# A list scheduler gets new costs: a shared memory port, other matmul steps, and a price for changing the array's form

## The chip, the cores and the metric

The kernel runs on one core of one Trainium2 chip. Five engines matter: TensorE (PE in the profile; its weight loads are PEld) multiplies matrices into PSUM, VectorE (DVE), ScalarE (ACT) and GpSimd (POOL) work element by element, and SyncE (SP) issues the transfers. The metric is the device time of one execution in microseconds. Times are medians of several runs.

## The reference

One layer of a hybrid decoder on 1024 prompt tokens and 8 x 4 sample tokens, 1056 columns in all, of width 1024, in float32:

- RMSNorm, then one input projection into q (8 heads of 64), k and v (2 heads of 64) and 512 channels for a state-space layer (S5).
- Sliding-window attention (window 128) with sinks and a relative bias, in eight blocks of 128 queries, each against its own and the previous block; the samples attend to a cache.
- S5: 32 groups of 16 channels drive a 64-dimensional diagonal complex state each; a scan over the positions; y = Re(C h) + D u; GELU and a half-GLU.
- RMSNorm of both parts, one output projection, residual; RMSNorm, an MLP of width 4096 with squared ReLU, residual; the final RMSNorm.

The outputs are y for all tokens, the new keys and values, and the new states.

## The kernel before

**Layout.** Activations are held with channels on the 128 partitions and the 1056 tokens along the row, so that a matmul takes a 128x128 weight tile and 352 token columns (`TB`). A float32 product is made of three float32r matmuls: each operand is split into a high and a low part, and high x high, high x low and low x high are summed in PSUM (`mm`, `mm3`). In the profile those are the groups `PS<-R,wh` and `PS<-R,wl`; the text calls them bulk matmuls. A weight tile `wr` (128x512) arrives by DMA, `weights` copies its high part to `wh` (ScalarE or VectorE) and puts the rest into `wl` (VectorE or GpSimd). There are two buffers of each. The other matmuls are plain float32 ones (two records each in the profile) or float32r ones of attention: transposes, score products (`64*128`), value products (`128*64`), the S5 tables, and sums over partitions for the norms.

**Stages.** The kernel is recorded in program order: x and its split, the attention and S5 tables, the input projections (`proj`, `proj_b`), S5 in four generators of eight groups (`s5`), attention (`att_sample`, `att_block`), the attention half of the output projection (`x2_first`), `gelu`, `glu`, the S5 half (`x2_last`), and the MLP (`up`, `down`) with the final norm. The string `SCRIPT` gives the order of record up to the MLP, a token for each piece: the two projections `b2` and `b3`, of 72 bulk matmuls each, stand among the attention steps `A`, with a negative `BOOST`, as fillers for TensorE.

**The planner.** What is recorded is not issued in that order. `Plan.record` notes each operation with its alternatives (an elementwise operation on SBUF tiles, `ew`, may go to VectorE or GpSimd; a copy, `copy`, to ScalarE or VectorE), a cost for each by `op_cost`, and its dependences. `Plan.schedule` then runs a list schedule: `prio` is the longest path of costs to the end; at each step every engine offers the operation that can start earliest (`s`, the later of the engine's free time and the operands' arrival), ties go to the higher priority, and the earliest of the engines' offers is placed. On TensorE, priorities are those of a group of matmuls, with 100 added for all that is not bulk. An operation with alternatives is left for another engine when that one would end it earlier, its waiting queue counted by half (`QW`). Buffers and PSUM banks are given out on the way. `Plan.issue` then writes the operations out in the planned order: each engine's queue is fixed, and only semaphores for true dependences and buffers hold it at run time. All planned operations are issued from one line, so the profile shows them as L339, and groups are told apart by tiles.

**What the planner assumes before the change.** VectorE and GpSimd never disturb each other. A bulk matmul of 352 columns costs 0.0025 + 352/2400 = 0.149 us; a plain one of 64 output rows and n columns 0.03 + n/1200; changing from one kind of matmul to another costs nothing. A VectorE operation of n elements costs 0.07 + n/960 us, a GpSimd one 0.15 + 0.0021 n, or 0.00166 n where an operand is broadcast.

**Names that the prediction uses.** GELU (`gelu`): per group a square, two products with (1 + tanh), one of 1024 and one of 32 columns a row in strided order, and the split. x2_first adds x to an accumulator `big` by `ett(acc[m], acc[m], xr, OP.add)`, a 128x1056 add for VectorE or GpSimd. In S5, the rotated states are put into a row `HA` together with the samples' start states (`pcopy`) and zeros (`ew.memset`), which the y^T products of 136 columns read.

Of the kernel before, what the change touches and what calls it, by code (L numbers as in the profile page):

```python
# [18 lines left out]
# ---------------------------------------------------------------- planning: the kernel is written in program order, its  # L19
# operations are recorded, and a list scheduler puts them in the order in which they are issued  # L20
# [17 lines left out]
class View:  # L38
    """part of a planned tile: the elements it covers, and how the real tile gives it"""
# [33 lines left out]
class Op:  # L73
    __slots__ = ("alts", "tiles", "succ", "ndep", "prio", "avail", "i", "table", "src", "why", "s", "boost", "bulk")


QW = 0.5
# [4 lines left out]
TABLE = {AF.Exp: 1, AF.Tanh: 1, AF.Sin: 2, AF.Sqrt: 3}  # L82


def op_cost(eng, method, args, kw):
    out = args[0]
    if eng == "SP":
        v = next((x for x in args if isinstance(x, View)), None)
        return max(0.1, (v.ix.size if v else math.prod(out.shape)) * 4 / 360e3)
    n = math.prod(out.ix.shape[1:])  # L90
    vs = [a for a in args if isinstance(a, View)]
    psum = any(a.tile.space == "PS" for a in vs)
    if eng == "PE":
        m = args[1].ix.shape[-1]
        if method == "transpose":
            return 0.109
        if args[1].dt == F32R:
            return 0.0025 + max(n, 256) / 2400
        if m <= 64:
            return max(0.06, 0.03 + n / 1200)  # L100
        return max(0.134, 0.0025 + n / 600)
    if eng == "ACT":
        aps = sum(isinstance(kw.get(k), View) for k in ("scale", "bias"))
        return (0.05 if psum else 0.093) + n / 1200 + 0.094 * aps + (0.095 if "accum_out" in kw else 0)
    if eng == "DVE":
        if method == "memset":
            return 0.05
        if method == "reciprocal":
            return 0.07 + n * 0.0062
        if method == "tensor_reduce":  # L110
            n = math.prod(args[1].ix.shape[1:])
        if method in ("tensor_scalar", "tensor_copy") and not psum:
            return 0.07 + n / 1920
        return (0.13 if psum and method == "scalar_tensor_tensor" else 0.07) + n / 960
    if method == "memset":
        return 0.04 + n / 3000
    if method == "tensor_scalar":
        return 0.16 + n / 1200
    bc = len(vs) < 3 or any(a.ix.strides[-1] == 0 for a in vs[1:])
    return 0.15 + n * (1.66 if bc else 2.1) / 1000  # L120


class Plan:
# [4 lines left out]
    # -- tiles  # L128
# [11 lines left out]
    # -- operations  # L140
# [3 lines left out]
    def record(self, calls):  # L144
        o = Op()
        o.i, o.boost, o.bulk = len(self.ops), self.boost, self.bulk
        o.alts = [(e, m, a, k, op_cost(e, m, a, k)) for e, m, a, k in calls]
        a, k = calls[0][2:]
# [3 lines left out]
        f = a[2] if len(a) > 2 else None  # L152
# [18 lines left out]
        if calls[0][0] == "PE":  # L171
            # accumulation groups of a bank stay in order
            v = a[0]
            key = v.box()[2] // 512
            prev = v.tile.last.get(key)
            if prev is not None and o.i not in prev.succ:
                prev.succ[o.i] = False
                o.ndep += 1
            v.tile.last[key] = o
# [7 lines left out]
    # -- the list scheduler  # L187
    def schedule(self):
# [5 lines left out]
        # a group of matmuls counts as its most urgent one  # L194
        group = {}
# [6 lines left out]
        table = [0]  # L202
        pend = {e: [] for e in ENG}
        units_end = {}
        phase_left = [sum(1 for t in self.tiles if t.left and t.phase == p) for p in (0, 1, 2)]
        # allocation: in the order of record among the tiles that compete for a unit
# [21 lines left out]
        def slot(t):  # L228
            """(time, units) of the best free place, or None"""
            if t not in heads[t.space] or (t.phase == 2 and phase_left[1]):  # L230
                return None
            best = None
            for c in t.cands:
                if all(live.get((t.space, u)) is None for u in c):
                    e = max(units_end.get((t.space, u), 0.0) for u in c)
                    if best is None or e < best[0]:
                        best = (e, c)
            return best
# [5 lines left out]
        def queue(e, o):  # L244
            """what is ahead of o on an engine"""
            return self.qw * sum(b[4] for q, b in pend[e] if q.prio > o.prio and q.avail <= free[e])
# [5 lines left out]
        while len(seq) < len(ops):  # L252
            best = None
            for e, lst in pend.items():
                cand = None
                fe = free[e]
                for o, a in lst:
                    s = max(fe, o.avail)
                    if cand is not None and s > cand[0] + 1e-9:
                        continue  # L260
                    if len(o.alts) > 1:
                        fin = s + a[4]
                        if any(b[0] != e and max(free[b[0]], o.avail) + b[4] + queue(b[0], o) < fin for b in o.alts):
                            continue
# [33 lines left out]
            if e == "SP":  # L298
                free[e] = s + 0.5
                dma[0] = max(dma[0], s + 0.5) + a[4]  # L300
                end = dma[0]
            else:
                c = a[4]
                if e == "ACT" and o.table and o.table != table[0]:
                    table[0] = o.table
                    c += 1.28
                end = free[e] = s + c
            for t in o.tiles:
# [22 lines left out]
    # -- issue  # L331
# [33 lines left out]
# rows: which ones a part of the kernel takes  # L365
# [6 lines left out]
# order of record up to the MLP  # L372
# [5 lines left out]
def body(tc, I, O, dbg=None):  # L378
# [14 lines left out]
    def copy(out, in_):  # L393
        """ScalarE or VectorE"""
        plan.record([("ACT", "activation", (out, in_, AF.Copy), {}), ("DVE", "tensor_copy", (out, in_), {})])
# [15 lines left out]
    with ExitStack() as ctx:  # L411
# [57 lines left out]
        # ------------------------------------------------------------ weights: four k-tiles of 128 columns at a time  # L469
# [8 lines left out]
        def mm(outs, w, xs, first, last, cols=tbs):  # L478
            """accumulates sum_k w[k]^T x[k]; three products carry float32"""
# [13 lines left out]
        # ------------------------------------------------------------ constants  # L493
# [11 lines left out]
        # ------------------------------------------------------------ norms: 1/sqrt(mean + eps), per token  # L505
        def rs_sum(ss, p, blocks, start=True, stop=True, b0=0, p0=0):
            """per-token mean of squares (ss summed over partitions), tokens on partitions"""
# [5 lines left out]
        def rs_calc(p, b0, b1, f, out, root=True, p0=0):  # L513
            """out[:, b] = (f sum + eps)^(-1/2), or ^(-1)"""
# [20 lines left out]
        def rs_row(r, row, b0=0, b1=9):  # L535
            """r[token] on all partitions, into a row"""
# [11 lines left out]
        # ------------------------------------------------------------ x: gain, split, squares  # L548
# [32 lines left out]
        # ------------------------------------------------------------ attention tables  # L581
# [36 lines left out]
        # ------------------------------------------------------------ S5 parameters, [(parity, p), pair]  # L618
# [26 lines left out]
        def s5_params():  # L645
# [55 lines left out]
            # (lambda_bar - 1) / lambda  # L701
# [17 lines left out]
            # b_bar and the block diagonal C  # L719
# [5 lines left out]
            # phase tables e^(i 8 theta n): n = 16 a + b  # L725
# [19 lines left out]
        # ------------------------------------------------------------ S5, eight groups (four pairs) at a time  # L745
# [7 lines left out]
        def u_part(ut, b, p):  # L753
            """tokens by s, then n, of 8 n + s; the samples' (i, b) at the end"""
# [12 lines left out]
        def s5(m, units, par):  # L767
            """rows (7 - s, c) of U hold token 8 n + s of channel c; par: rows it is given"""
# [5 lines left out]
            # lambda^s b_bar  # L774
# [9 lines left out]
            # kernel K[tau], its Toeplitz form by way of DRAM; F by transposes  # L784
# [19 lines left out]
            # phase table  # L804
# [6 lines left out]
            # G: Re(C lambda^(t+1)), -Im  # L811
# [25 lines left out]
            # X = F^T U; rotate  # L837
# [47 lines left out]
            # scan  # L885
# [8 lines left out]
            # rotate back  # L894
# [18 lines left out]
            # y^T  # L913
# [19 lines left out]
        # ------------------------------------------------------------ input projection  # L933
# [29 lines left out]
        def in_first(ms):  # L963
            """as x arrives"""
# [14 lines left out]
        def proj_b(m):  # L979
            """by token blocks"""  # L980
# [8 lines left out]
        def kv_tokens():  # L989
            """token-major k (last 128 and sample) and v"""  # L990
# [20 lines left out]
        # ------------------------------------------------------------ attention  # L1011
# [11 lines left out]
        def softmax(S):  # L1023
            """exponentials and their sums"""
# [6 lines left out]
        def probs(S, dn):  # L1031
            """normalized and transposed"""
# [123 lines left out]
        # ------------------------------------------------------------ output projection, residual  # L1156
        ms = [None] * 8

        def o_split(i):
            """o with its gain, in two parts of tokens"""  # L1160
# [27 lines left out]
        # ------------------------------------------------------------ GELU, GLU  # L1188
# [74 lines left out]
        # ------------------------------------------------------------ up to the MLP, in this order  # L1263
# [24 lines left out]
        # ------------------------------------------------------------ MLP; the norm's 1/(mean + eps) comes after the square  # L1288
# [37 lines left out]
        # the last chunk by token blocks, the final norm behind it  # L1326
# [141 lines left out]
```

## Time and profile before

| | us |
|---|---|
| median of 3 runs | 1217.54 |
| lowest, highest | 1208.55, 1219.12 |
| span of the profiled execution, first to last instruction | 1209.6 |
| TensorE busy in it | 1153.0 (95%) |
| VectorE busy | 670.9 (55%) |
| ScalarE busy | 274.2 (23%) |
| GpSimd busy | 277.0 (23%) |

The profile is of one execution; the page gives its span, and no other time of its own. Busy shares are means over the whole span, and the stages differ: the first third holds projections, S5 and attention, the rest the MLP. A busy TensorE is not one at its peak, since matmuls overlap; the granted clock (PEclk, a share of full speed) has two levels, 1.2 and 2.4 GHz, and a mean between 0.5 and 1 tells how the stretch was divided. A name such as `R` stands for a row buffer of 128x1088, `big` for the accumulators, `PS` for PSUM, `t` for a 128x512 scratch, `sx` for small softmax sums. The arrow in a wait points from the waiting instruction to the engine and tile that ended the wait.

### The profile page before, as it was taken

The page shows a single profiled execution, that of the slowest core. Times are in us where ns is not written, and L with a number is a line of the kernel's source. Part 1 is how long each engine was busy: PE and PEld are TensorE (multiplying, and loading weights), DVE is VectorE, ACT ScalarE, POOL GpSimd, SP SyncE. Part 2 cuts the span into 40 slices and gives each one's busy share as a digit, 9 for nine tenths or more (in the row PEclk, how much of TensorE's full clock was granted, in tenths as well). Part 3 has the DMA queues.
Part 4 walks back from the last instruction along what each step waited for, and adds up shares of the span by engine and source line. Part 5 has one row for each costly group of instructions (what it writes and reads, how often), then busy time and mean ns, then how long its engine had stood idle before and what let it go on. Part 6 is the DMA issues. An engine that isn't in the chain of part 4 may idle for free.

```text
span 1209.6 us, 17482 instructions
## 1 busy us (share of the span) xinstructions
PE 1153.0 (95%) x7231; PEld 1109.0 (92%) x7231; DVE 670.9 (55%) x970; ACT 274.2 (23%) x512; POOL 277.0 (23%) x259
## 2 busy tenths in 40 slices
PE   6989999979888999999999999999999999999997
PEld 6888996658778999999999999999999999999996
DVE  8687747898789894522522533432432432534575
ACT  4212134632143321211111111111111111111241
POOL 4066414575463140020010010010011011000011
PEclk9989989969889999999999999999999999999997
DMA  6312320023331111111211111111111211121212
GB/s 234 102 47 71 98 46 11 9 47 93 85 99 44 37 44 43 44 44 44 53 44 45 53 44 36 52 44 44 53 44 45 53 44 44 44 52 44 79 54 92
DMA packets 55711, 69.71 MB, mean 58 GB/s; under 512 B 12184, under 2 KB 31808, under 8 KB 55616
## 3 DMA queue, kind: packets, MB, share of 16 engines
q1 hardware_dynamic: 55632, 68.59, 20.3%
q8 instruction: 57, 0.93, 0.4%
q14 instruction: 22, 0.18, 0.0%
HBM read 58.96 MB, written 6.15 MB: 54 GB/s over the span
## 4 chain that ended last, share of the span: by engine, by line
PE 69%; DVE 3%; ACT 1%; issue 0%; DVEq 0%; ACTq 0%; POOL 0%
PE PS L339 69%; DVE R L339 2%; DVE big L339 1%; ACT P L339 1%; ACT wh L339 0%; ACT R L339 0%; DVE wl L339 0%; DVE rsc L339 0%; DVE wh L339 0%; DVEq L1464 0%; ACT rsc L339 0%; ACTq L339 0%; DVE rs L339 0%; POOL R L339 0%; DVEq L339 0%
## 5 line engine op out<-in xcount | busy, mean ns | idle before, releaser
L339 PE MATMUL PS<-R,wh 128*128 128x352 f32 x3840 | 749.2, 326 | 19.4 <-DVE wh L339 10.1
L339 PEld LDWEIGHTS PS<-R,wh 128*128 128x128 f32 x3840 | 643.2, 191 | 25.6 <-DVE wh L339 10.5
L339 PE MATMUL PS<-R,wl 128*128 128x352 f32 x1920 | 430.1, 326 | 0.9 <-POOL wl L339 0.5
L339 PEld LDWEIGHTS PS<-R,wl 128*128 128x128 f32 x1920 | 331.5, 191 | 4.8 <-issue 2.1
L339 POOL TENSOR_TENSOR wl<-wr,wh 128x512 fp32r<-128x512 f32 x64 | 92.7, 1449 | 700.2 <-ACT wh L339 490.0
L339 ACT ACTIVATE wh<-wr 128x512 fp32r<-128x512 f32 x144 | 91.0, 632 | 649.9 <-PE PS L339 637.4
L339 DVE TENSOR_TENSOR wl<-wr,wh 128x512 fp32r<-128x512 f32 x96 | 70.2, 731 | 255.4 <-ACT wh L339 249.9
L339 DVE TENSOR_TENSOR big<-PS,big 128x1056 f32<-128x1056 f32 (+2 forms) x80 | 82.5, 1035 | 167.0 <-PE PS L339 166.9
L339 PE MATMUL PS<-R,R 128*128 128x384 f32 (+9 forms) x816 | 140.8, 342 | 19.1 <-DVE R L339 8.4
L339 PEld LDWEIGHTS PS<-R,R 128*128 128x128 f32 (+3 forms) x816 | 111.3, 196 | 40.2 <-POOL R L339 15.4
L339 DVE TENSOR_TENSOR R<-R,R 64x508 f32<-64x508 f32 (+8 forms) x55 | 44.6, 823 | 4.9 <-ACT R L339 4.3
L339 POOL TENSOR_TENSOR R<-R,R 128x512 f32<-128x512 f32 (+6 forms) x34 | 39.3, 1163 | 32.6 <-DVE R L339 23.9
L339 DVE TENSOR_TENSOR P<-P 128x1056 f32<-128x1056 f32 x32 | 40.3, 1259 | 6.6 <-ACT P L339 6.6
L339 DVE TENSOR_TENSOR P<-P,R 128x1056 f32<-128x1056 f32 x32 | 40.4, 1263 | 0.9
L339 DVE TENSOR_TENSOR R<-P,R 128x1056 fp32r<-128x1056 f32 x32 | 40.3, 1258 | 1.1
L339 ACT ACTIVATE R<-PS 128x512 f32<-128x512 f32 (+3 forms) x40 | 22.6, 570 | 75.9 <-PE PS L339 70.0
L339 ACT ACTIVATE P<-PS 128x1056 f32<-128x1056 f32 (+2 forms) x35 | 34.6, 988 | 8.8 <-PE PS L339 8.8
L339 ACT ACTIVATE R<-R 128x352 f32<-128x352 f32 (+4 forms) x32 | 25.8, 823 | 38.8 <-DVE R L339 38.5
L339 DVE SCALAR_TENSOR_TENSOR R<-R,R 128x352 f32<-128x352 f32 (+5 forms) x28 | 32.2, 1186 | 1.3 <-ACT R L339 1.3
L339 ACT ACTIVATE R<-R,sx 128x129 f32<-128x129 f32 x68 | 26.5, 392 | 22.7 <-DVE sx L339 22.7
L339 ACT ACTIVATE P<-big 128x384 f32<-128x384 f32 (+2 forms) x29 | 19.1, 662 | 50.5 <-DVE big L339 46.1
L339 POOL TENSOR_TENSOR big<-big,R 128x1056 f32<-128x1056 f32 x7 | 25.8, 3680 | 10.1 <-DVE big L339 9.9
(140 smaller groups left out, 691.1 us busy)
## 6 DMA issues: line engine op xcount, KB each, us to landing
wr<-in_w_up_dram SPq DMA_DIRECT2D x64, 256.0 KB
wr<-in_w_down_dram SPq DMA_DIRECT2D x64, 256.0 KB
R<-in_xT_dram SPq DMA_DIRECT2D x15, 528.0 KB
wr<-in_w_in_dram SPq DMA_DIRECT2D x20, 256.0 KB
wr<-in_w_out_dram SPq DMA_DIRECT2D x16, 256.0 KB
out_y_dram<-big SPq DMA_DIRECT2D x8, 384.0 KB
R<-R SPq DMA_DIRECT2D x32, 68.0 KB
R<-R SPq DMA_DIRECT2D x32, 64.0 KB
```

The costliest lines, as they stand in the source:

```text
L339: getattr(engines[e], m)(*[res(x) for x in args], **{k: res(x) for k, x in kw.items()})
```

## The change

Comments and docstrings are taken out, so that later line numbers shift. Beyond that only the planner is changed; what is recorded, `SCRIPT`, `BOOST` and the buffers stay.

- `op_cost`: new figures for matmuls, for GpSimd's two-input operations, and a factor of 1.87 on a VectorE operation with an operand whose elements lie 8 or more apart (`far`).
- `port`: says whether an operation takes the port that VectorE and GpSimd share: every GpSimd operation but a memset; on VectorE those with two SBUF inputs, the scan, and copies and scalar operations from SBUF to SBUF. `record` notes it (`o.port`), and `schedule` starts such an operation no earlier than the other engine's last such operation ends (`held`), also where it compares alternatives.
- `form`: rows and columns of the array that a matmul's stationary operand takes, rounded up to 32, 64 or 128. A matmul whose form differs from that of the one placed before it starts 0.2 us later in the plan (`SWITCH`).

```diff
-QW = 0.5
+QW, SWITCH = 0.5, 0.2
...
+def far(v):
+    st = [abs(b) for n, b in zip(v.ix.shape, v.ix.strides) if n > 1]
+    return bool(st) and st[-1] >= 8 * v.ix.itemsize
+
+def form(args):
+    up = lambda n: 32 if n <= 32 else 64 if n <= 64 else 128
+    return up(args[1].ix.shape[0]), up(args[1].ix.shape[-1])
...
         if args[1].dt == F32R:
-            return 0.0025 + max(n, 256) / 2400
+            return max(0.056, 0.0133 + n / 2400)
         if m <= 64:
-            return max(0.06, 0.03 + n / 1200)
-        return max(0.134, 0.0025 + n / 600)
+            return max(0.107, n / 600)
+        return max(0.224, 0.013 + n / 600)
...
-        return (0.13 if psum and method == "scalar_tensor_tensor" else 0.07) + n / 960
+        slow = 1.87 if any(far(a) for a in vs) else 1.0
+        return (0.13 if psum and method == "scalar_tensor_tensor" else 0.07) + n / 960 * slow
...
-    bc = len(vs) < 3 or any(a.ix.strides[-1] == 0 for a in vs[1:])
-    return 0.15 + n * (1.66 if bc else 2.1) / 1000
+    return 0.16 + n * 1.75 / 1000
+
+def port(eng, method, args):
+    if method == "memset" or eng not in ("DVE", "POOL"):
+        return False
+    if eng == "POOL":
+        return True
+    big = [a for a in args[1:] if isinstance(a, View) and a.ix.size > a.ix.shape[0]]
+    sb = [a for a in big if a.tile.space != "PS"]
+    if method in ("tensor_scalar", "tensor_copy"):
+        return len(sb) == len(big) and args[0].tile.space != "PS"
+    return len(sb) > 1 or method == "tensor_tensor_scan"
...
+        o.port = {c[0] for c in calls if port(c[0], c[1], c[2])}
+        o.form = form(calls[0][2]) if calls[0][0] == "PE" else None
...
+        held = {"DVE": 0.0, "POOL": 0.0}
+        other = {"DVE": "POOL", "POOL": "DVE"}
+        shape = [None]
...
                     s = max(fe, o.avail)
+                    if e in o.port:
+                        s = max(s, held[other[e]])
+                    if e == "PE" and o.form != shape[0]:
+                        s += SWITCH
...
-                        if any(b[0] != e and max(free[b[0]], o.avail) + b[4] + queue(b[0], o) < fin for b in o.alts):
+                        if any(b[0] != e and max(free[b[0]], o.avail, held[other[b[0]]] if b[0] in o.port else 0.0) + b[4]
+                               + queue(b[0], o) < fin for b in o.alts):
...
                 end = free[e] = s + c
+                if e in o.port:
+                    held[e] = end
+                if e == "PE":
+                    shape[0] = o.form
```

## Rows read from the trace of the kernel before

**Rows 1.** Table by stretches: us, each engine's busy time (instructions), granted clock, DMA share, GB/s.
```profile
0.00:160.00 160.00, 139.96 (x933) 133.52 (x936) 117.31 (x265) 43.59 (x63) 69.62 (x106) 0.95 0.38 108
160.00:270.00 110.00, 100.90 (x640) 73.21 (x622) 88.76 (x154) 50.55 (x179) 55.51 (x50) 0.88 0.10 25
270.00:393.00 123.00, 105.19 (x646) 98.83 (x642) 105.50 (x130) 36.51 (x57) 59.59 (x43) 0.91 0.31 79
393.00:1183.80 790.80, 790.03 (x4929) 787.51 (x4930) 346.01 (x390) 139.19 (x205) 88.02 (x58) 1.00 0.17 47
1183.80:1209.60 25.80, 16.88 (x115) 15.98 (x114) 13.29 (x33) 4.40 (x10) 4.22 (x4) 0.73 0.30 107
```

**Rows 2.** Waits of TensorE, 0 to 393 us: us in total, times, longest.
```profile
PE PS L339 <- POOL R L339: 13.2, 7, 6.0
PE PS L339 <- DVE R L339: 11.6, 7, 4.5
PE PS L339 <- DVE wh L339: 10.1, 2, 5.7
```

**Rows 3.** VectorE's groups by shape, 0 to 393 us: count, busy us, mean ns, idle before.
```profile
L339 DVE TENSOR_TENSOR R<-R,R 128x512 f32<-128x512 f32 x13 | 15.0, 1185 | 0.0
L339 DVE SCALAR_TENSOR_TENSOR R<-R,prm,R 128x1056 fp32r<-128x1056 f32 x7 | 14.5, 2091 | 0.1
L339 DVE TENSOR_TENSOR t<-L,R 128x512 f32<-128x512 f32 x11 | 13.6, 1239 | 0.2
L339 DVE SCALAR_TENSOR_TENSOR R<-R,R 128x32 f32<-128x32 f32 x4 | 9.6, 2403 | 0.0
L339 DVE TENSOR_TENSOR R<-PS,R 128x512 f32<-128x512 f32 x12 | 7.5, 677 | 0.0
```

**Rows 4.** GpSimd's groups by shape, 0 to 393 us.
```profile
L339 POOL TENSOR_TENSOR big<-big,R 128x1056 f32<-128x1056 f32 x7 | 25.8, 3680 | 10.1 <-DVE big L339 9.9
L339 POOL TENSOR_TENSOR R<-R,cst 128x512 f32<-128x512 f32 x14 | 19.2, 1375 | 13.1 <-ACT R L339 9.5 <-DVE R L339 2.0 <-DVE sx L339 1.5
L339 POOL TENSOR_TENSOR R<-R,sx 128x512 f32<-128x512 f32 x12 | 14.9, 1242 | 21.0 <-DVE sx L339 21.0
```

**Rows 5.** VectorE's groups by shape, 450 to 1150 us.
```profile
L339 DVE TENSOR_TENSOR R<-wr,R 128x512 fp32r<-128x512 f32 x6 | 4.1, 689 | 0.1
```

**Rows 6.** Order of time, 0 to 32 us: start us, us, engine, operation, count.
```profile
10.15 1.32 DVE L339 SCALAR_TENSOR_TENSOR R<-R,prm,R 128x1056 fp32r<-128x1056 f32 x1
...
14.60 7.04 DVE L339 SCALAR_TENSOR_TENSOR R<-R,prm,R 128x1056 fp32r<-128x1056 f32 x3
...
14.83 3.41 POOL L339 TENSOR_TENSOR R<-R,R 128x1056 f32<-128x1056 f32 x1 [13.61 <-DVE R L339]
```

**Rows 7.** Order of time, 330 to 366 us, VectorE, then GpSimd.
```profile
333.97 4.51 DVE L339 SCALAR_TENSOR_TENSOR R<-R,R 128x1024 f32<-128x1024 f32 x2
339.70 1.26 DVE L339 TENSOR_TENSOR R<-R,R 128x1056 fp32r<-128x1056 f32 x1 [1.21 <-ACT R L339]
...
334.11 4.30 POOL L339 TENSOR_TENSOR big<-big,R 128x1056 f32<-128x1056 f32 x1
```

**Rows 8.** Order of time, 304 to 320 us.
```profile
311.51 3.29 POOL L339 TENSOR_TENSOR R<-R,R 128x512 f32<-128x512 f32 x2 [1.94 <-DVE R L339]
...
316.19 1.25 PE L339 MATMUL PS<-R,R 128*128 128x136 f32 x4 [6.00 <-POOL R L339]
```

**Rows 9.** Order of time, TensorE, 186 to 200 us and 296 to 304 us.
```profile
188.12 0.32 PE L339 MATMUL PS<-R,wh 128*128 128x352 f32 x1
188.37 4.32 PE L339 MATMUL PS<-R,R 64*128 64x256 f32 x26
192.62 0.43 PE L339 MATMUL PS<-R,wh 128*128 128x352 f32 x1
192.88 0.48 PE L339 MATMUL PS<-R,wl 128*128 128x352 f32 x2
...
298.34 1.97 PE L339 MATMUL PS<-R,R 128*64 128x128 f32 x32
```

More of the change, by code (lines that the diff above doesn't have):

```diff
@@ L73 @@
 class Op:
-    __slots__ = ("alts", "tiles", "succ", "ndep", "prio", "avail", "i", "table", "src", "why", "s", "boost", "bulk")
-QW = 0.5
+    __slots__ = ("alts", "tiles", "succ", "ndep", "prio", "avail", "i", "table", "src", "why", "s", "boost", "bulk", "port", "form")
+QW, SWITCH = 0.5, 0.2
 ENG = ("PE", "ACT", "DVE", "POOL", "SP")
```

## The prediction

> **What bounds the kernel now.** I read the table by stretches first, because the page's shares are a mean over unlike stages [rows 1]. From 393 to 1183.8 us, the MLP, TensorE is busy 790.03 of 790.80 us at full clock while VectorE is busy for 346 and GpSimd for 88: nothing that reorders those two can shorten it. The last 25.8 us are the final norm. Before 393 us TensorE is busy for 139.96 + 100.90 + 105.19 = 346 us, so 47 us are idle; VectorE is busy there for 312 us and GpSimd for 185. That stage is held by no single engine but by chains that cross from VectorE and GpSimd to TensorE. The granted clock in it is 0.88 to 0.95 of full, so some of it runs at the lower of the two levels. Second, the waits of TensorE before 393 us name what it waits for: rows written by GpSimd 13.2 us, by VectorE 11.6 us, and VectorE's weight copies 10.1 us, 34.9 together [rows 2]; of the last, 5.7 are the wait for the first weights and 4.4 come later. Third, the groups by shape show why they are late. A VectorE subtraction of two 128x512 SBUF tiles takes 0.689 us where GpSimd is quiet [rows 5], but the same shape averages 1.185 and 1.239 us before 393 us, while one that reads an operand from PSUM stays at 0.677 [rows 3]. A GpSimd 128x1056 add takes 3.680 us on average, a 128x512 product 1.375 or 1.242 [rows 4]. So the two engines hold each other up when both read SBUF and VectorE reads two tiles of it, and a PSUM reader is free of it. The start shows it plainly: one VectorE split of 128x1056 takes 1.32 us alone, three take 7.04 us once a GpSimd add of 3.41 us has begun [rows 6], and the 4.4 us wait of TensorE follows.
>
> **The change, part by part.** No instruction's arithmetic changes; the planner's costs do, and with them the order on each queue and the choice of engine where two are allowed.
>
> *The port.* In the plan, a VectorE instruction with two SBUF inputs and a GpSimd one may no longer overlap, so GpSimd is chosen only when VectorE is in a PSUM reader or a reduction, waits, or has a queue. Moving everything off GpSimd would not pay. The first three rows of VectorE [rows 3] exceed their quiet price by 13 x 0.50 + 7 x 0.77 + 11 x 0.55 = 18 us, with 0.689 us from [rows 5] and 1.32 from [rows 6]; the fourth is four small instructions of 2.40 us, each of which has less to do than the 0.677 us PSUM reader of sixteen times its width, so at least 4 x 1.7 = 7 us more. Against these 25 us, the GpSimd groups of [rows 4] alone would cost VectorE 7 x 1.26 + 26 x 0.69 = 27 us if all were moved (1.26 us is a 128x1056 subtraction [rows 7]). So the total is about a wash, and the gain lies in where they are put. I take it site by site, each capped by the idle time of TensorE there.
> - GELU, 333 to 367 us: four times VectorE needs about 4.5 us for two instructions, the second of which stands behind a GpSimd 128x1056 add of 4.30 us; then VectorE is idle for 1.21 us while ScalarE works [rows 7]. In that gap VectorE would do the add in 1.26 us. That frees at most 4 x 2.2 = 9 us of VectorE's chain, ends 0 and 9; TensorE's idle time from 270 to 393 us is 123.00 - 105.19 = 17.8 us [rows 1], 6.0 of them the next site's. I take 6.
> - 310 to 316 us: TensorE waits 6.00 us for rows that GpSimd writes last, and GpSimd's queue holds two 128x512 products of 3.29 us together ahead of those small pieces [rows 8]. On VectorE, or earlier in the queue, that goes; VectorE's own instructions for the same rows are late next. Ends 0 and 6: I take 3.
> - Attention, 160 to 270 us: 110.00 - 100.90 = 9.1 us idle [rows 1], with VectorE busy 88.8 us. Ends 0 and 9; I take 3, since a third of TensorE's waits of [rows 2] is on GpSimd's rows.
> - Up to 160 us: of the 4.4 us I take 2, since VectorE then does the three sums of squares itself at 1.26 us each and x still has to arrive; of the other idle time I take 1. Ends 0 and 4.4.
>
> *The step prices.* A bulk matmul of 352 columns takes 790.80 / 4929 = 0.160 us in the MLP [rows 1]. The planner's price goes from 0.149 to 0.160, so that its TensorE no longer runs ahead of the real one. This alone removes nothing; I count it as part of the sites above.
>
> *The form price.* The planner adds 0.2 us to the start of a matmul that uses other rows or columns of the array than the last one. In the trace a bulk matmul just after a change takes 0.26 us to the next (192.62 to 192.88), and one just before a change 0.25 (188.12 to 188.37) [rows 9], against 0.160: 0.10 us on the bulk side of each, and if the other side pays as much, the 0.2 is right. These rows hold two changes in 4.8 us, 0.4 us of 4.8. If half are saved over the 110 us of attention, that is 4.6 us of TensorE's time; TensorE is not the only bound there, so I take 3, ends 0 and 5.
> But the price is added to the start, and the planner takes the earliest start ahead of the highest priority. So a bulk matmul that is ready goes ahead of any score or value product of another form, and the +100 that put the non-bulk ones first no longer works across forms. The fillers that are spread through attention now (two projections of 72 matmuls, 72 x 0.160 = 11.5 us each) may be spent ahead of it. What waits behind is the softmax work on VectorE and ScalarE. That costs from 0 to 23 us. VectorE has 21 us of slack in that stretch [rows 1], which hides most; I take 4 us lost.
> The trace shows 32 records, two for each of 16 matmuls of a 64-column form, in 1.97 us, 0.12 us a matmul [rows 9], where the new price says 128/600 = 0.213: the plan will think TensorE busy 16 x 0.09 = 1.5 us longer in each such group than it is, one reason for the 4 us. The Trainium skill's page TensorEngine Tiling (Key Properties) says that different tiles of the array can work in parallel, and this row agrees; it speaks against a price that sums them.
>
> *The clock.* The means of 0.88 from 160 to 270 us and 0.91 from 270 to 393 [rows 1] are 0.24 x 110 + 0.18 x 123 = 49 us at the lower level, which cost up to 24 us (an estimate from the two levels). Ends: 5 lost where fillers are gone, 10 won. I take 2 won.
>
> *MLP and tail.* The engines' shares may change; TensorE's 790 us of work cover it, and without that cover nothing is left to gain, since the engines that feed it are idle for half of the time. In the tail GpSimd is busy for 4.22 us [rows 1]; ends 2 lost and 2 won, I take 0.
>
> Sum: 6 + 3 + 3 + 2 + 1 + 3 - 4 + 2 = 16 us less. The page gives a span of 1209.6 us for the profiled execution and nothing of what lies around it; that is 7.9 us below the median of the runs, 1217.54, which spread from 1208.55 to 1219.12. From the span the sum gives 1194; from the median, for which the prediction is, 1217.5 - 16 = 1202 us.
>
> **Rivals.**
> *No difference, 1205 to 1222 us.* The plan's exclusion is only an order on two queues: no semaphore holds GpSimd back while VectorE is in a two-input instruction. Where real times leave the plan by one short instruction, the port goes to whoever comes first, as at the start [rows 6], and GpSimd's pieces are as late as now. Against it: at the GELU site the same collision comes four times in the same order [rows 7], so it is a planned one. With half of the 20 us won above and the 4 lost, it is 6 us less: 1211. The Trainium skill's page SBUF — State Buffer (Who interferes with whom) says that the issue order decides who blocks, and that the other waits for the whole instruction; the 7.04 us row agrees. By that rule a plan that is off by one place gives nothing. That GpSimd simply keeps all its work belongs here too.
> *Slower, 1222 to 1236 us: bulk matmuls starve attention.* Place: the score products from 160 us on. If both fillers, 23 us, run before them, VectorE has no softmax work for that long, and later TensorE has no filler between score and value products, stands idle and falls to the lower clock. Price: 23 lost + 5 of clock, less 15 won at the other sites = 13 us more, 1230. It decides from the point where more than 15 us of bulk run in one piece with score inputs ready. For it: the rule of start before priority is plain in the code. Against: bulk needs weights, whose low parts come from VectorE or GpSimd, and that breaks the bulk runs whenever VectorE is full; it is 81% busy there.
>
> **How the numbers follow.** Forecast (1183 to 1205) 0.50, no difference 0.31, slower 0.19. One per cent, 12 us, is about what can be told from no change here. The low end takes away all the 34.9 us of [rows 2]: 1217.5 - 34.9 = 1183. The high end is the slower case's own time, 1230; beyond the two lie 0.05 and 0.14. Faster by over 1% (below 1205.4): 0.50; within: 0.35; slower (above 1229.7): 0.15.
>
> **What would show it.** Right: GpSimd's busy time before the MLP falls from 185 us toward 120, 128x512 subtractions and products of SBUF tiles on VectorE come near 0.69 us, the small GELU instructions of 2.40 us fall below 1, TensorE's wait for rows of GpSimd falls below 6 us, and the unbroken MLP begins 12 us or more earlier, with its length the same. Wrong: those fall but the MLP begins at the same time (then the waits have only changed names, most likely to VectorE's rows), or bulk runs of over 10 us stand ahead of score products and VectorE's busy share in attention falls below 75%, or a difference appears inside the MLP, which no step above allows.

## The result: 56 us slower, and the profile after

The changed kernel takes 1270.42 us (median) against 1214.23 us: ratio 1.0464, 95% interval 1.0406 to 1.0522. It was forecast at 1202, with 1183 to 1230 as the range. One of its four executions took 2266.39 us, its bulk matmuls 0.32 us apart (the last section); it is left out of the ratio, and the profile below is of the changed kernel run once more (1265.62 us, span 1263.8).

The table by stretches of the changed kernel, columns as in [rows 1]. Its third stretch ends with the last matmul that sums the squares ahead of the MLP, at 447.2 us; in the kernel before that matmul ends at 397.9.

```profile
0.00:160.00 160.00, 127.11 (x822) 119.12 (x822) 101.21 (x284) 41.65 (x58) 20.03 (x49) 0.89 0.31 97
160.00:270.00 110.00, 89.60 (x560) 76.77 (x562) 68.28 (x130) 31.01 (x102) 31.28 (x31) 0.78 0.14 32
270.00:447.20 177.20, 144.62 (x896) 124.97 (x892) 139.13 (x229) 66.86 (x151) 32.64 (x30) 0.89 0.25 64
447.20:1240.00 792.80, 782.00 (x4851) 779.80 (x4851) 328.00 (x364) 156.93 (x219) 80.09 (x56) 0.99 0.15 46
1240.00:1263.80 23.80, 14.34 (x108) 13.38 (x107) 12.52 (x36) 2.79 (x7) 1.54 (x2) 0.77 0.32 117
```

Of the 54 us between the two spans (1263.8 and 1209.6), 49 have been lost by that matmul. From there to the end of the MLP the changed kernel takes 792.8 us where the one before takes 785.9 (397.9 to 1183.8). Right behind that matmul TensorE waits 2.77 and 1.65 us, for the norm's factors and what is made with them, with no bulk matmul left; inside the MLP, at 561.05 us, it has waited another 6.39 us until ScalarE has written `P` from PSUM. The tail is 2 us shorter. The order of time for TensorE from 446 to 456 us and at 561 us in the changed kernel, and from 397 to 404 us in the one before:

```profile
447.00 0.22 PE L378 MATMUL PS<-ones_k,R 128*32 128x1 f32 x2
450.00 3.74 PE L378 MATMUL PS<-ident,rs 128*128 128x128 f32 x18 [2.77 <-DVE rs L378]
455.38 0.95 PE L378 MATMUL PS<-R,wh 128*128 128x352 f32 x2 [1.65 <-DVE P L378]
...
561.05 2.13 PE L378 MATMUL PS<-R,wh 128*128 128x352 f32 x6 [6.39 <-ACT P L378]
```

```profile
397.86 1.06 PE L339 MATMUL PS<-R,wh 128*128 128x352 f32 x5
398.76 0.65 PE L339 MATMUL PS<-R,wl 128*128 128x352 f32 x3
399.25 1.12 PE L339 MATMUL PS<-R,wh 128*128 128x352 f32 x6
```

The loss is idle time. Over the whole span TensorE is busy for 1157.7 us, against 1153.0 before, and idle for 106.1 against 56.6: 50 us more idle, 5 more busy. The granted clock ahead of the MLP is lower (0.89, 0.78, 0.89 against 0.95, 0.88, 0.91). Both kernels do the same 7231 matmuls, so what the lower level costs, less what fewer changes of form may save, is within the 5 us. GpSimd, busy for 185 us before 393 us, is busy for 20.03 + 31.28 + 32.64 = 84 up to 447 us.

TensorE's waits from 0 to 449 us (us in total, times, longest), against [rows 2]:

```profile
PE PS L378 <- DVE R L378: 31.9, 17, 7.4
PE PS L378 <- ACT R L378: 13.2, 7, 5.2
PE PS L378 <- DVE sx L378: 12.6, 2, 7.8
PE PS L378 <- DMA R<-kd: 9.1, 1, 9.1
PE PS L378 <- DVE wh L378: 5.4, 1, 5.4
PE PS L378 <- POOL R L378: 3.1, 2, 2.9
```

The wait for GpSimd's rows is down from 13.2 us to 3.1, and those for VectorE's rows, for ScalarE, for softmax sums (`sx`) and for the Toeplitz rows that come by DMA (`kd`) have grown or are new: chains that began too late. VectorE's and GpSimd's groups by shape from 0 to 449 us, against [rows 3] and [rows 4]:

```profile
L378 DVE TENSOR_TENSOR R<-R,R 128x512 f32<-128x512 f32 x20 | 14.8, 774 | 0.0
L378 DVE TENSOR_TENSOR t<-L,R 128x512 f32<-128x512 f32 x22 | 14.6, 695 | 2.8 <-DMA out_nks_dram<-t 2.7
L378 DVE SCALAR_TENSOR_TENSOR R<-R,prm,R 128x1056 fp32r<-128x1056 f32 x7 | 9.2, 1317 | 2.5 <-ACT R L378 2.4
...
L378 DVE SCALAR_TENSOR_TENSOR R<-R,R 128x32 f32<-128x32 f32 x4 | 1.0, 241 | 0.0
...
L378 POOL TENSOR_TENSOR R<-R,cst 128x512 f32<-128x512 f32 x11 | 14.5, 1320 | 41.3 <-ACT R L378 29.6 <-PE PS L378 11.6
L378 POOL TENSOR_TENSOR big<-big,R 128x1056 f32<-128x1056 f32 x3 | 7.4, 2452 | 28.7 <-DVE big L378 28.7
L378 POOL TENSOR_TENSOR R<-R,sx 128x512 f32<-128x512 f32 x3 | 3.1, 1042 | 3.5 <-DVE sx L378 3.5
```

The three shapes that averaged 1.185, 1.239 and 2.091 us take 0.774, 0.695 and 1.317, and the small GELU instruction 0.241 in place of 2.403: for these shapes the port model does on the chip what it says. The large GELU instruction does not follow: it averages 2.737 us, against 2.189 before; one of its four still meets a GpSimd add (shown further down). What replaced the collisions stands in the chain of waits (start us, us, what):

```profile
92.06 31.42 PE PS L378 x197
123.48 2.96 issue
126.45 0.63 ACT wh L378
...
128.55 7.92 DVE R L378 x17
...
172.91 3.85 DMA R<-kd
```

From 92 us TensorE does nothing but bulk matmuls, then VectorE's S5 work and a DMA stand on the chain, with little left for TensorE to do beside them. The stretch from 92 to 126 us by engine, the changed kernel and then the one before:

```profile
92.00:126.00 34.00, 33.95 (x214) 33.94 (x214) 10.61 (x17) 5.98 (x8) 7.69 (x6) 1.00 0.21 65
```

```profile
92.00:126.00 34.00, 30.54 (x273) 28.52 (x273) 26.14 (x43) 7.01 (x14) 20.09 (x29) 0.93 0.26 66
```

VectorE is busy for 10.6 us of 34 where it was busy for 26.1. The first S5 products of 64 output rows start at 126.77 us in the changed kernel, and at 92.08 in the one before. Rows of TensorE from there to the first score product (`64*128`) in the changed kernel, and the two ends in the kernel before:

```profile
126.77 1.97 PE L378 MATMUL PS<-R,big 128*64 128x128 f32 x32
...
138.29 3.59 PE L378 MATMUL PS<-R,R 128*128 128x32 f32 x16 [7.38 <-DVE R L378]
149.54 3.68 PE L378 MATMUL PS<-R,R 128*64 128x128 f32 x32 [1.16 <-DMA R<-R]
...
159.99 5.20 PE L378 MATMUL PS<-R,big 128*128 128x136 f32 x23 [3.50 <-DVE R L378]
...
191.81 2.51 PE L378 MATMUL PS<-R,R 64*128 64x128 f32 x24
```

```profile
92.08 2.44 PE L339 MATMUL PS<-R,big 128*64 128x128 f32 x32
...
160.70 2.50 PE L339 MATMUL PS<-R,R 64*128 64x128 f32 x24
```

They weren't late for want of an operand. Their stationary operand `big` is written by two copies of 128x512, one on ScalarE at 91.25 us and this one on VectorE, which ends at 93.45; the transfers of the other operand are issued by 86.7. By these rows the products could have started some 30 us sooner:

```profile
92.76 0.69 DVE L378 COPY big<-PS 128x512 f32<-128x512 f32 x1 [0.75 <-PE PS L378]
```

What stands ahead of them can be counted in the traces: 576 bulk matmuls, as many as eight projections of 72, where the kernel before has 353. The 223 more are 36 us at 0.160 us each, and the products start 35 us later. That work isn't saved behind them. From the first S5 product to the first score product only 48 bulk matmuls are left, where the kernel before has 240, and yet the stretch is only 4 us shorter (65.0 us against 68.6): TensorE's work doesn't set its length. From 126.77 to 183.36 us TensorE has no bulk matmul at all and is idle for 26 of 57 us, at a granted clock of 0.67; in as long a stretch from its first S5 product on, the kernel before is idle for 4:

```profile
126.77:183.36 56.59, 30.62 (x293) 27.85 (x292) 42.46 (x96) 7.16 (x17) 9.15 (x15) 0.67 0.26 61
```

```profile
92.08:148.67 56.59, 52.23 (x402) 49.96 (x401) 44.63 (x74) 9.70 (x19) 30.90 (x44) 0.96 0.33 83
```

There each small product waits in the open for the step before it. From the first score product to the matmul that ends the third stretch the changed kernel takes 255 us against 237, so the 49 us are 35 ahead of S5, 4 won in it and 18 behind. The two fillers `b2` and `b3` are not what was spent: from 160 to 270 us the changed kernel has 144 bulk matmuls and the one before 127.

### The profile page after: what moved, and what is told of

Read it like the earlier page. It is cut to its first block, busy times and chain, and to the rows that moved or that the text cites. A ratio compares the mean times of both kernels' runs of the same rounds, so it can differ in the third digit from the quotient of the medians.

```text
span 2264.6 us, 17429 instructions
## 1 busy us (share of the span) xinstructions
PE 2182.3 (96%) x7231; PEld 1971.7 (87%) x7231; DVE 643.3 (28%) x1038; ACT 303.4 (13%) x536; POOL 164.1 (7%) x167
## 3 DMA queue, kind: packets, MB, share of 16 engines
q1 hardware_dynamic: 55632, 68.59, 10.6%
## 4 chain that ended last, share of the span: by engine, by line
PE 95%; DVE 3%; SPq 1%; ACT 1%; DMA 0%; issue 0%; POOL 0%; DVEq 0%; ACTq 0%
PE PS L378 95%; DVE R L378 2%; SPq L378 1%; ACT R L378 0%; DVE P L378 0%; DVE t L378 0%; DMA R<-in_xT_dram 0%; DVE sx L378 0%; DMA R<-kd 0%; DVE big L378 0%; ACT L378 0%; ACT P L378 0%; DVE rsc L378 0%; POOL R L378 0%; DMA out_nks_dram<-t 0%
## 5 line engine op out<-in xcount | busy, mean ns | idle before, releaser
L378 PE MATMUL PS<-R,wh 128*128 128x352 f32 x3840 | 1386.3, 529 | 22.8 <-ACT P L378 6.2
L378 PEld LDWEIGHTS PS<-R,wh 128*128 128x128 f32 x3840 | 1142.3, 303 | 123.0 <-issue 42.0
L378 PE MATMUL PS<-R,wl 128*128 128x352 f32 x1920 | 765.6, 528 | 0.0
L378 PEld LDWEIGHTS PS<-R,wl 128*128 128x128 f32 x1920 | 571.5, 302 | 47.5 <-issue 20.3
L378 PE MATMUL PS<-R,R 128*128 128x384 f32 (+9 forms) x816 | 230.4, 525 | 22.6 <-DVE R L378 12.9
L378 PEld LDWEIGHTS PS<-R,R 128*128 128x128 f32 (+3 forms) x816 | 178.3, 296 | 63.9 <-issue 35.8
L378 POOL TENSOR_TENSOR wl<-wr,wh 128x512 fp32r<-128x512 f32 x55 | 70.5, 1282 | 1419.4 <-PE PS L378 1274.3
L378 DVE TENSOR_TENSOR R<-R,R 128x512 f32<-128x512 f32 (+8 forms) x72 | 48.9, 696 | 1.4 <-ACT R L378 0.9
L378 PE MATMUL PS<-ident,R 128*128 128x128 f32 x110 | 28.5, 435 | 18.0 <-DVE sx L378 8.5
L378 ACT ACTIVATE R<-PS 128x512 f32<-128x512 f32 (+4 forms) x44 | 24.4, 555 | 145.7 <-PE PS L378 145.3
L378 DVE SCALAR_TENSOR_TENSOR R<-R,R 128x352 f32<-128x352 f32 (+5 forms) x28 | 24.8, 909 | 26.3 <-ACT R L378 26.1
```

The source lines that it names most:

```text
L378: getattr(engines[e], m)(*[res(x) for x in args], **{k: res(x) for k, x in kw.items()})
```

## The experiments

Ratios are to the kernel before on the same chip, with 95% intervals; medians in us. On the chips of these runs the kernel before has medians from 1212.64 to 1218.71 us, and on one of them its executions spread over 1% (1209.25 to 1220.09). Differences between runs are therefore taken from the ratios.

### Which part of the change

**after_again**: no edit.

> The changed kernel unaltered, to see where its 56 us go (1270.4 us median against 1214.2). Form theory (the price added to the start of a matmul of another form lets bulk matmuls run ahead of everything else): bulk runs of over 30 us stand ahead of the score products, the MLP begins 45 to 60 us later than at 393 us, and its length is 790 us as before. Port theory (GpSimd's work is moved to VectorE, which then bounds the stage): the MLP also begins that much later, but VectorE is over 90% busy from 160 us to the MLP. Costs theory (the new step prices alone reorder): late MLP with neither of the two signs.

1265.62 us; the rows above. A run of 31.42 us of bulk, and 49 us lost ahead of the MLP, as the form theory has it. VectorE is 62% busy from 160 to 270 us, so the port theory's sign is missing. A long bulk run is no sign by itself: the kernel before has one of 21 us from 59.6 us on. What is new is that S5 products which could start stand behind one.

**a_noform**
```diff
-QW, SWITCH = 0.5, 0.2
+QW, SWITCH = 0.5, 0.0
```


> The change with the form price at 0, port and step prices kept. Form theory: all of the 56 us come back, 1195 to 1217 us, and if the port model is worth the 10 us and more that was forecast for it, below 1205. Port theory: stays at 1260 to 1272. Costs theory: stays at 1255 to 1272.

1219.19, ratio 1.0040 (1.0014 to 1.0067). Some 51 of the 56 us come back, which leaves it just above the form theory's range. It isn't faster than before, so port and new costs together gain nothing.

**b_form**: the kernel before, with `form` and the price as the change has them.
```diff
+                    if e == "PE" and o.form != shape[0]:
+                        s += SWITCH
```


> The kernel before with the form price of 0.2 us alone. Form theory: 1255 to 1280 us, nearly the whole loss. Port theory and costs theory: 1205 to 1220, no difference.

1295.74, ratio 1.0662 (1.0600 to 1.0725). The price alone costs 80 us, more than any theory said, so the parts of the change don't simply add. Its table for 0 to 393 us, and that of the kernel before:

```profile
0.00:393.00 393.00, 320.06 (x1988) 285.82 (x1989) 282.76 (x513) 103.54 (x257) 157.58 (x186) 0.83 0.24 70
```

```profile
0.00:393.00 393.00, 346.04 (x2189) 305.56 (x2189) 311.57 (x548) 130.65 (x298) 184.72 (x197) 0.92 0.28 76
```

All four engines have got less done by 393 us, TensorE 200 matmuls less: a chain is late, no engine is full.

**a_noport**
```diff
-        o.port = {c[0] for c in calls if port(c[0], c[1], c[2])}
+        o.port = set()
```


> The change without the port model (no operation takes it), form price and step prices kept. Form theory: 1260 to 1285 us, as slow as the change or slower by what the port model wins. Port theory: back to 1205 to 1220. Costs theory: 1255 to 1275.

1298.88, ratio 1.0695 (1.0623 to 1.0766). This is above every range: the port model is worth about 28 us in the change's company, and the port theory falls.

### What in the form price

**a_form002**
```diff
-QW, SWITCH = 0.5, 0.2
+QW, SWITCH = 0.5, 0.02
```


> The change with a form price of 0.02 us in place of 0.2. If the rule does the harm (any price on the start puts a ready bulk matmul ahead of every priority), a tenth of the price costs nearly as much: 1245 to 1275 us. If the size does it (matmuls put off by what the price says), 1217 to 1226, a tenth of the way from the change without it (1219).

1259.57, ratio 1.0345 (1.0316 to 1.0374). A tenth of the price keeps 37 of the 51 us: the rule does most of it, and the size the rest.

**a_formtime**
```diff
-                    if e == "PE" and o.form != shape[0]:
-                        s += SWITCH
...
+                if e == "PE" and o.form != shape[0]:
+                    c += SWITCH
                 end = free[e] = s + c
```


> The change with the same 0.2 us, but added to the duration of a matmul of another form once it has been chosen, and left out of the start by which it is chosen. If the rule does the harm: 1205 to 1225 us, as without the price (1219) or a little better, since TensorE's plan is then truer. If to know the price at all does it: over 1240.

1209.20, ratio 0.9929 (0.9900 to 0.9957). The same 0.2 us, known to the plan but not to the choice, is slightly faster than before.

**a_formbulk**
```diff
-                    if e == "PE" and o.form != shape[0]:
+                    if e == "PE" and o.bulk and o.form != shape[0]:
```


> The change with the form price of 0.2 us on the start of bulk matmuls alone; the others start unpriced. If the harm is that ready bulk matmuls go ahead of score, value and S5 products: 1200 to 1224 us, as without the price (1219). If any price on a start does harm, whichever kind waits: over 1240.

1209.88, ratio 0.9954 (0.9933 to 0.9976). With the price on the start of bulk matmuls alone, the loss is gone: the harm is in the price on the starts of the others. That it was bulk they stood behind is what the traces show. The first S5 products start at 91.00 us in a_noform, 91.51 in a_formtime and 91.66 here, near the 92.08 of the kernel before, with 388 to 390 bulk matmuls ahead of them. They start at 126.77 us in the change, 131.15 in a_form002, 140.45 in b_form and 144.31 in a_noport, and in each of these four 576 bulk matmuls go first. The four runs that lost over 40 us have this, and the other three don't.

### The port model and the costs apart

**b_port**: the kernel before, with `port`, `held` and both places that use it.
```diff
+                    if e in o.port:
+                        s = max(s, held[other[e]])
```


> The kernel before with the port model alone: costs and form price as before. Forecast theory (the port model takes TensorE's waits away at GELU, the start and attention): 1198 to 1208 us, and the step prices took it back in the change without form price (1219). Its rival (a wash: the waits change names): 1210 to 1222.

1205.88, ratio 0.9909 (0.9878 to 0.9941): 11 us gained, in the range of the forecast theory. TensorE's waits from 0 to 393 us:

```profile
PE PS L360 <- DVE R L360: 26.9, 15, 4.9
PE PS L360 <- DVE wh L360: 5.2, 1, 5.2
PE PS L360 <- DMA R<-kd: 3.2, 1, 3.2
PE PS L360 <- ACT R L360: 3.0, 5, 1.2
PE PS L360 <- POOL R L360: 1.6, 2, 1.3
```

GpSimd's 13.2 us of [rows 2] have shrunk to 1.6 and the later of the two waits for weight copies is gone, while the wait for VectorE's rows has grown from 11.6 to 26.9. So the rival is half right: most of the waiting has changed its name, and TensorE's idle time up to 393 us falls only from 47 to 41 us.

**b_costs**: the kernel before with the new `op_cost` and `far`.

> The kernel before with the new costs alone (matmul steps, strided operands, GpSimd): no port, no form price. If the costs take back what the port wins: 1222 to 1240 us. If neither matters: 1208 to 1222.

1236.37, ratio 1.0157 (1.0122 to 1.0192): they take 19 us, more than the port model gives. Together the two make 8 us lost, and a_noform measured 5.

**c_64**, one new cost alone
```diff
-            return max(0.06, 0.03 + n / 1200)
+            return max(0.107, n / 600)
```


> The kernel before with one new cost alone: a float32 matmul with at most 64 output rows is priced max(0.107, n/600) in place of max(0.06, 0.03 + n/1200). The new costs together took 19 us (1236 against 1218.7). If this price does it, since it sums matmuls that run side by side: 1228 to 1242. If another cost does it: 1210 to 1224.

1222.01, ratio 1.0053 (1.0023 to 1.0083): 6 us, and so another cost does most of it.

**c_no64**: b_costs with that line as before.

> The kernel before with all the new costs but that one. If that price did the harm: 1208 to 1222. If the others did it: 1228 to 1242.

1244.09, ratio 1.0220 (1.0178 to 1.0262), just above the higher range. The price that the prediction blamed isn't the culprit: without it, the others cost at least as much (the intervals of this run and of b_costs overlap).

**a_formtime_old64**: a_formtime with that line as before.

> The change with the form price in the duration (1209 us alone) and the old price for 64 output rows. If that price takes 10 us or more back: 1190 to 1203. If it does not: 1204 to 1216.

1218.45, ratio 1.0013 (0.9990 to 1.0036): 10 us worse than a_formtime, outside both ranges. Here the old price is the worse one, in c_64 it was the new one.

**c_bulk**
```diff
-            return 0.0025 + max(n, 256) / 2400
+            return max(0.056, 0.0133 + n / 2400)
```


> The kernel before with one new cost alone: the float32r matmul, 0.160 us for 352 columns in place of 0.149, and 0.067 in place of 0.109 for 128. Without the price for 64 rows the new costs took 27 us (1244 against 1217). If a truer bulk step is what upsets the order (TensorE's plan gets longer, bulk work moves ahead or behind): 1230 to 1248. If not: 1210 to 1224.

1226.48, ratio 1.0100 (1.0038 to 1.0163), between the two ranges.

**c_m128**
```diff
-        return max(0.134, 0.0025 + n / 600)
+        return max(0.224, 0.013 + n / 600)
```


> The kernel before with one new cost alone: a float32 matmul of more than 64 output rows, 0.224 us at least in place of 0.134. If this does it: 1230 to 1248. If not: 1210 to 1224.

1221.59, ratio 1.0050 (1.0019 to 1.0081), in the lower range.

**c_ew**: `far`, its factor, and GpSimd's 0.16 + 0.00175 n alone.

> The kernel before with the new costs of VectorE (strided operands) and GpSimd alone: a GpSimd product of 512 columns 1.056 us in place of 1.225, so that without the port model it looks cheaper and GpSimd gets more. If this does it: 1230 to 1248, with GpSimd busier before the MLP than 185 us. If not: 1210 to 1224.

1228.00, ratio 1.0117 (1.0062 to 1.0173), between the two ranges; GpSimd is busy for 192 us up to 393 us, so a little more than 185. All four lose, 6 to 14 us each, none the whole.

**c_bulkdown**
```diff
-            return 0.0025 + max(n, 256) / 2400
+            return max(n, 256) / 2400 - 0.0083
```


> The kernel before with the bulk step moved the other way, 0.138 us for 352 columns in place of 0.149, further from the measured 0.160. If the order of record was settled with the old prices and any departure loses: 1221 to 1235 us, as with 0.160 (1226). If the direction matters (a longer step upsets, a shorter one helps): 1200 to 1216.

1234.93, ratio 1.0162 (1.0127 to 1.0197), as any departure would have it.

**c_ewup**
```diff
-    return 0.15 + n * (1.66 if bc else 2.1) / 1000
+    return 0.15 + n * (1.95 if bc else 2.45) / 1000
```


> The kernel before with GpSimd's price moved the other way, 0.15 + 0.00245 n (0.00195 n with a broadcast operand), 1.404 us for 512 columns in place of 1.225. If any departure loses: 1221 to 1235 us. If the direction matters (a cheaper GpSimd gets too much while the port isn't modelled): 1200 to 1216, with GpSimd less busy before the MLP than 185 us.

1219.58, ratio 1.0048 (1.0024 to 1.0073), between the two ranges, with GpSimd busy for 163 us up to 393 us. The first of the two moves a price away from the measured 0.160 us. The second moves one past it: where VectorE stands idle beside them, GpSimd operations on two full 128x512 operands take 1.27 to 1.28 us in the kernel before. Both lose.

### The two gains together

**b_port_formtime**: b_port with the form price in the duration, all costs as before.

> The kernel before with the port model, as in the run at 1206, and the form price in the duration; all costs as before. In the change, to move the form price from absent to the duration was worth 10 us (1219 to 1209). If the two gains add: 1192 to 1202. If each only reshuffles the order: 1200 to 1215, no better than the port model alone.

1193.10, ratio 0.9814 (0.9762 to 0.9866): the fastest of all, 23 us under the kernel before. Its table for 0 to 393 us and TensorE's largest waits there:

```profile
0.00:393.00 393.00, 361.32 (x2322) 319.79 (x2323) 322.53 (x680) 142.93 (x317) 62.19 (x85) 0.92 0.28 78
```

```profile
PE PS L371 <- DVE R L371: 14.6, 12, 4.2
PE PS L371 <- DVE wh L371: 5.5, 1, 5.5
PE PS L371 <- DMA R<-R: 5.2, 1, 5.2
```

TensorE does 2322 matmuls by 393 us where the kernel before does 2189, and is idle for 32 us instead of 47; GpSimd is busy for 62 us.

## Why the prediction was wrong

**The step that failed** is in the form price: "That costs from 0 to 23 us. VectorE has 21 us of slack in that stretch [rows 1], which hides most; I take 4 us lost." The mechanism was named: the planner takes the earliest start ahead of the priority, so a ready bulk matmul goes first and the +100 no longer works. Its size was wrong by more than ten times: 51 us between a_noform and the change, 80 alone. Three things were missed.
- *The place.* I looked at attention and its two fillers. The rule holds from the first matmul, and what it spends is the projections ahead of S5: 576 bulk matmuls stand before the first S5 product in place of 353, and it starts at 126.77 us in place of 92.08, long before the first score product. The 23 us that bounded the cost counted only `b2` and `b3`, and those two still stand in attention.
- *The brake.* That the need for weights "breaks the bulk runs whenever VectorE is full" did not hold, because VectorE, starved of S5 work, is not full: 10.6 us of 34. Starving feeds itself.
- *The slack.* VectorE's 21 us idle in attention can't be used by work that isn't there yet. Late chains then ran without bulk beside them, which is the 50 us of idle time: 26 from 126.77 to 183.36 us alone, where the kernel before has 4 in as long a stretch. Of the lower clock, for which the rival had 5 us, no more than that is seen.

The slower rival said 13 us more at 0.19. It was the right case at the wrong place and price, and the end of the range at 1230 was its own price. The prediction also let no difference appear inside the MLP; the 6.39 us wait at 561.05 us is one. That four of the five signs of being right came true (GpSimd's time, the two-tile shapes, the small GELU instruction, the wait for GpSimd's rows) while the time went the other way is because they are signs of the port model alone.

**The port model was right in kind and near in size.** The sites won 6 + 3 + 3 + 2 + 1 = 15 us in the sum; alone it measures 11 (b_port), and no run tells the sites apart. GpSimd's time fell further than the 120 us foretold, to 84, and TensorE's wait for its rows to 3.1 us. At the GELU site the pair of VectorE instructions that took 4.51 us [rows 7] takes about half that where GpSimd keeps out, and 4.57 us where a GpSimd add is still in the way. Two of the four groups in order of time on VectorE, and the add on GpSimd:

```profile
396.16 4.57 DVE L378 SCALAR_TENSOR_TENSOR R<-R,R 128x1024 f32<-128x1024 f32 x2
400.56 1.25 DVE L378 TENSOR_TENSOR big<-big,R 128x1056 f32<-128x1056 f32 x1
...
406.11 2.06 DVE L378 SCALAR_TENSOR_TENSOR R<-R,R 128x1024 f32<-128x1024 f32 x2
408.04 1.25 DVE L378 TENSOR_TENSOR big<-big,R 128x1056 f32<-128x1056 f32 x1
```

```profile
396.10 2.46 POOL L378 TENSOR_TENSOR big<-big,R 128x1056 f32<-128x1056 f32 x1
```

In the second, the add that stood in GpSimd's queue is one of VectorE's, 1.25 us, right behind the pair, in the place that the site's working gave it. The first is the rival's case: `held` keeps such a pair and such an add apart in the plan, and on the chip they met. It happened in one of four groups here, and didn't undo the gain in b_port.

**The step prices** were said to remove nothing, and the new prices of VectorE and GpSimd had no term at all. Together they cost 19 us (b_costs), and those of VectorE and GpSimd alone 14 (c_ew). Nor are all of them truer: 0.213 us for 64 output rows overstates the trace's 0.12, and 1.056 us for a GpSimd operation on 512 columns is further from the 1.27 to 1.28 us above than the old 1.225 (it fits the 1.05 us that one with a broadcast operand takes undisturbed). The remark on the 64-row price fell all the same: a_formtime_old64 is slower without it, and c_no64 no faster. What the six runs with one price changed have in common is that each is slower, truer or not, up or down, three of them by only 0.5%. This fits an order of record and boosts that were settled with the old prices; that is an inference from six cases, and no run here settled `SCRIPT` anew.

**The gain of fewer form changes** (3 us) isn't seen by itself: counted in the traces, the changes of form fall from 142 to 98, and TensorE is still busy for 5 us longer. A gain from the price in the duration is seen: 1.1% (a_noform at 1.0040 to a_formtime at 0.9929), 13 us, and 1.0% (b_port at 0.9909 to b_port_formtime at 0.9814), 12 us. Fewer changes don't explain it: they go from 140 to 122 and from 150 to 144, at 0.2 us each 3.6 and 1.2 us. Whether the plan is better because its TensorE is truer, or the order merely fell well, is open; single prices moved the time by as much without becoming truer.

## What to carry to other kernels

In a list scheduler that takes the earliest start first, a price added to a start is a priority above all priorities, and 0.02 us of it kept 37 of the 51 us that 0.2 cost; here the loss went away with the price in the duration, and with the price on the bulk work alone. Bound such a step by all the work that the rule can let pass, over the whole schedule, not by the stretch in which the trace shows the contest. A truer price need not make a faster plan (c_bulk set one to the measured 0.160 us and lost 1.0%); the hand-made order beside it may be the reason, which no run here shows. Change one price at a time, and measure each.

## What the runs showed of the hardware

One execution of the changed kernel ran for 2266 us with the same program that takes 1270 us. From 1200 to 1400 us of it the table shows 624 bulk matmuls in 200 us, 0.32 us each, twice the 0.160 of the MLP in [rows 1]. Nowhere in that execution do two bulk matmuls start less than 0.26 us apart, where 0.16 is the rule in the repeat; TensorE was busy for 96% of the whole, and its page has no line of granted clock at all:

```profile
1200.00:1400.00 200.00, 200.00 (x624) 184.34 (x623) 38.60 (x39) 16.48 (x22) 8.96 (x7) 1.00 0.09 24
```

The 1.00 in this row is thus no proof of full speed; the step of the matmuls is. Why the engine showed no sign of the higher level in that execution isn't known, and it came once.
